# Seven block products in half of the gate/up pieces of a decoder trunk, and low parts made by accumulating transfers

## The chip, the cores and the metric

The kernel runs on one core of one Trainium2 chip. The metric is the device time of one execution in microseconds (us), the median of three runs. Five engines work side by side, each on its own instruction queue: TensorE (matmuls), VectorE, ScalarE, GpSimd (POOL) and SyncE (SP, which here only issues DMAs). Sixteen DMA engines serve the queues of all of them.

## The reference, cut to what matters

Two layers over 256 tokens of width 2048. Layer 0 mixes with a diagonal state-space scan and a gated linear unit, layer 1 with sliding-window attention. Each is followed by a SwiGLU block, which is where the change lies:

```python
def swiglu(x, w_gate, w_up, w_down):
    return (jax.nn.silu(x @ w_gate) * (x @ w_up)) @ w_down
...
        h = h + mix
        hn = rmsnorm(h, norm_ffn[i])
        h = h + swiglu(hn, ffn_w_gate[i], ffn_w_up[i], ffn_w_down[i]).astype(h.dtype)
```

The inner width is 5632. All is float32.

## The kernel before, in words

**Three matmuls for one product.** Every operand is split into a high part, rounded to the matmul's reduced float32 (`F32R`), and a low part, the rest. `products` adds high x high, high x low and low x high into one PSUM bank (L926, L927, L928), 128 x 128 by 128 x 512 each. A *piece* is a block of weights of 512 rows by 512 columns, 1 MB. It takes 4 row blocks x 2 blocks of 128 tokens x 3 = 24 matmuls. The program has 332 pieces: 32 of the gated linear unit, 36 of attention's projections, 88 for gate, 88 for up, 88 for down.

**How a piece gets ready.** The class `Weights` holds the pieces in the order of use. When TensorE's code takes piece i (`next`), the pieces up to i+2 are split and up to i+4 loaded. A load is one DMA issued by SP (L109) into one of two buffers `raw`. `high` (L122) is one ScalarE instruction that writes the rounded copy into a buffer `w`, of which there are three, so a piece's buffer is that of the piece three before it. `low` (L127) is one VectorE subtraction, raw minus high.

**The FFN.** The 5632 inner columns go in 11 chunks of 512. For a chunk, four pieces of gate are multiplied, then four of up (the first chunk alternates between them, so that the last quarter of the normed activations is wanted late). ScalarE applies the gate's function, VectorE multiplies by up, and the result is turned (32 x 32 block transposes on VectorE, `blocks_turned`, L1007) and split into high and low for the down product; each layer's last chunk is turned by TensorE instead. Chunks come in groups of three, and the group's down product (4 blocks of output columns) stands after the first chunk of the next group.

**Order.** Instructions are issued to each engine by a list scheduler which simulates the program and takes what is ready; the code's order is the priority. Work that can be deferred is put into the list `left` and taken out between pieces. PSUM has eight banks, each one accumulator of 128 x 512.

Of the kernel before, what the change touches and what calls it, by code (L numbers as in the profile page):

```python
# [9 lines left out]
F32 = mybir.dt.float32  # L10
# [7 lines left out]
P = 128  # L18
# [4 lines left out]
EPS = 1e-6  # L23
FF = 5632
FFC = FF // 512
FF_GROUPS = ((0, 1, 2), (3, 4, 5), (6, 7, 8), (9, 10))

G = 128
NS = 64
# [27 lines left out]
def kernel(  # L57
# [9 lines left out]
    def nm(s):  # L67
        uid[0] += 1
        return f"{s}_{uid[0]}"
# [10 lines left out]
    def bank(shape, name="ps"):  # L80
        return ps.tile(shape, F32, tag="ps", name=nm(name))
# [5 lines left out]
    def normed_tile(name):  # L87
        return wp.tile([P, 2, 4, T], F32R, tag="xt", name=nm(name), bufs=4)


    class Weights:
        def __init__(self):
            self.src, self.raw, self.hl = [], [], []
            self.early = {}
            self.third = None
            self.used = 0
            self.limit = 0

        def add(self, ap):
            self.src.append(ap)  # L100

        def load(self, upto):
            while len(self.raw) < min(upto, len(self.src)):
                i = len(self.raw)
                if i in self.early:
                    t = self.early[i]()
                else:
                    t = pp.tile([P, 4, 512], F32, tag="raw", name=nm("raw"), bufs=2)
                nc.sync.dma_start(t, self.src[i].rearrange("(a p) n -> p a n", p=P))  # L109
                self.raw.append(t)  # L110

        def place(self, i):
# [12 lines left out]
        def low(self, i, keep=lambda ins: ins, e=V):  # L125
            hi, lo = self.hl[i]
            keep(e.tensor_tensor(lo, self.raw[i], hi.bitcast(F32), op=ALU.subtract))  # L127

        def split(self, upto):
# [17 lines left out]


    TWO_ORDER = [(n, q) for n in (0, 1) for q in range(3)] + [(0, 3), (1, 3)]

    def add_ffn(i):
        def gu(c):
            pairs = [(w, q) for w in (w_gate, w_up) for q in range(4)]
            if c == 0:
                pairs = [((w_gate, w_up)[n], q) for n, q in TWO_ORDER]
            for w, q in pairs:
                W.add(w[i, 512 * q : 512 * (q + 1), 512 * c : 512 * (c + 1)])

        def down(g):
            for n in range(NCH):  # L160
                for c in FF_GROUPS[g]:
                    W.add(w_down[i, 512 * c : 512 * (c + 1), 512 * n : 512 * (n + 1)])

        ffn_order(gu, down)

    def ffn_order(gu, down):
        done = 0
        for g, chunks in enumerate(FF_GROUPS):
            for n, c in enumerate(chunks):
                gu(c)  # L170
                if n == 0 and g > 0:
                    down(g - 1)
        down(len(FF_GROUPS) - 1)
# [815 lines left out]
    def block_tile():  # L989
        return bt_tile().rearrange("p a b -> p (a b)")[:, : 4 * T].rearrange("p (a t) -> p a t", a=4)  # L990
# [3 lines left out]
    def through_dram(o, v):  # L994
# [3 lines left out]
            nc.gpsimd.dma_start(d[t].rearrange("(q k) e -> k q e", q=4), v[32 * t : 32 * t + 32])  # L998
        nc.gpsimd.dma_start(o, d.rearrange("t p e -> p t e"))

    def blocks_turned(o, v, tb):


        src = v[32 * tb : 32 * tb + 32].rearrange("p t (a c) -> p t a c", a=4)
        dst = o.rearrange("p a (t k) -> p t a k", t=2)
        for q in range(4):
            V.transpose(dst[32 * q : 32 * q + 32, :, :, 32 * tb : 32 * tb + 32],  # L1007
                        src[:, :, :, 32 * q : 32 * q + 32])

    class Norm:  # L1010
# [15 lines left out]
        def chunk(self, n, t):  # L1026
            self.square(n, t)
            if t == 1 and n in self.blocks:
                o, v = normed_tile("xT"), block_tile()
                self.xt[n] = o  # L1030
                left.extend(partial(blocks_turned, v, h[:, n], tb) for tb in range(4))

                def split():
                    gc = gcol[:, self.g, 4 * n : 4 * n + 4]
                    for a in range(4):
                        S.activation(o[:, 0, a], v[:, a], AF.Copy, scale=gc[:, a : a + 1])
                        V.scalar_tensor_tensor(o[:, 1, a], v[:, a], gc[:, a : a + 1], o[:, 0, a].bitcast(F32),
                                               ALU.mult, ALU.subtract)

                left.append(split)  # L1040
            elif t == 1 and n in self.through:
                left.extend(self.late)
                v, land = block_tile(), wp.tile([P, 2, 512], F32, tag="act", name=nm("act"), bufs=2)
                o = self.xt[n] = normed_tile("xT")
                V.transpose(v.rearrange("p a t -> p (a t)").rearrange("p (q t a k) -> p t a q k", q=4, t=2, a=4),  # L1045
                            h[:, n].rearrange("p t (a q k) -> p t a q k", a=4, q=4))
                through_dram(land.rearrange("p t c -> p (t c)").rearrange("p (b e) -> p b e", b=4),
                             v.rearrange("p a t -> p (a t)").rearrange("p (q e) -> p q e", q=4))

                lv = land.rearrange("p t c -> p (t c)").rearrange("p (b t a k) -> p b t a k", b=4, t=2, a=4)  # L1050

                def split():
                    gc = gcol[:, self.g, 4 * n : 4 * n + 4]
# [12 lines left out]
            elif t == 1:  # L1066
                left.extend(self.late)
                left.append(lambda: self.xt.__setitem__(n, normed(n, self.g)))

        def scale(self):  # L1070
            s = wp.tile([P, 2], F32, tag="ss", name=nm("ss"), bufs=2)
# [30 lines left out]
    def glu(norm):  # L1102
# [5 lines left out]
        for c in range(NCH):  # L1108
# [11 lines left out]
            for t in range(2):  # L1120
# [4 lines left out]
                V.tensor_tensor(hc, hc, sg, op=ALU.add)  # L1125
                norm.chunk(c, t)

    def swiglu(norm, out_norm):
        ht = {}
        r = [None]  # L1130

        def turned(c, hm):
            o = turned_tile("hT")
            for t in range(2):
                pt = bank([P, 4, P], "tr")
                for a in range(4):
                    PE.transpose(pt[:, a], hm[:, t, a * P : (a + 1) * P], ident)
                ts_ = slice(t * P, (t + 1) * P)
                S.copy(o[:, 0, :, ts_], pt)  # L1139
                V.tensor_tensor(o[:, 1, :, ts_], pt, o[:, 0, :, ts_].bitcast(F32), op=ALU.subtract)  # L1140
            ht[c] = o

        def gu(c):
            last = c == FF_GROUPS[-1][-1]
            if c == 0:
                pg, pu = two_linear(norm.xt)
                r[0] = norm.scale()
            else:
                pg = linear(norm.xt)
            sg = wp.tile([P, 2, 512], F32, tag="act", name=nm("act"), bufs=2)  # L1150
            for t in range(2):
                S.activation(sg[:, t], pg[t], AF.Silu, scale=r[0][:, t : t + 1])
            if c > 0:
                pu = linear(norm.xt)
            for t in range(2):
                V.scalar_tensor_tensor(sg[:, t], pu[t], r[0][:, t : t + 1], sg[:, t], ALU.mult, ALU.mult)
            if last:
                left.append(lambda: turned(c, sg))
                return
            o, v = turned_tile("hT"), block_tile()  # L1160
            ht[c] = o
            left.extend(partial(blocks_turned, v, sg, tb) for tb in range(4))

            def split():
                S.activation(o[:, 0], v, AF.Copy)  # L1165
                V.tensor_tensor(o[:, 1], v, o[:, 0].bitcast(F32), op=ALU.subtract)

            left.append(split)

        def down(g):  # L1170
            xt = Later(ht, FF_GROUPS[g])
            for n in range(NCH):
                last = out_norm.g is None and g == len(FF_GROUPS) - 1 and n == NCH - 1
                acc = linear(xt, len(FF_GROUPS[g]), halves=last)
                for t in range(2):
                    hc = h[:, n, t]
                    V.tensor_tensor(hc, hc, acc[t], op=ALU.add)  # L1177
                    if g == len(FF_GROUPS) - 1:
                        out_norm.chunk(n, t)

        ffn_order(gu, down)

    class Later:
        def __init__(self, d, keys):
# [2 lines left out]
        def __getitem__(self, i):  # L1187
            return self.d[self.keys[i]]

    def attention(norm, out_norm):  # L1190
        with tc.tile_pool(name="at", bufs=1) as ap:

            ji = ap.tile([P, 384], I32, name="ji")
# [153 lines left out]
            for n in range(NCH):  # L1347
                acc = accs[n] if n < 2 else linear(ot, 4)
                for t in range(2):
                    hc = h[:, n, t]  # L1350
                    V.tensor_tensor(hc, hc, acc[t], op=ALU.add)
                    out_norm.chunk(n, t)


    accs = []
# [9 lines left out]

    h = wp.tile([P, NCH, 2, 512], F32, name="h")

    n0 = Norm(0, (0, 1, 2, 3))
    glu(n0)
    n1 = Norm(1, (), (0, 1, 2, 3))  # L1370
    swiglu(n0, n1)
    n2 = Norm(2, (0, 1, 2, 3))
    attention(n1, n2)
    swiglu(n2, Last(None))


_INS = ["x", "norm_mix", "s5_a_re", "s5_a_im", "s5_log_step", "s5_b_re", "s5_b_im", "s5_c_re", "s5_c_im",
# [25 lines left out]
```

## Time and profile before

| | |
|---|---|
| median of 3 runs | 1981.72 us (1980.31 to 1982.71) |
| span of the profiled execution | 1976.9 us |
| median less that span | 4.8 us |
| TensorE busy | 1935.3 us |
| VectorE busy | 1287.2 us |
| ScalarE busy | 859.9 us |
| moved by DMA | 374.23 MB, mean 189 GB/s |
| mean granted TensorE clock | 0.993 |

The span runs from the first to the last instruction of one execution; the run's own time has a few us around it. Busy times are sums of instruction durations on an engine; matmuls overlap in their pipeline, so TensorE's busy time says only when it had work, and the rate is read from how many start in a stretch. Idle time of an engine that is not the bottleneck costs nothing by itself.

### The profile page before, as it was taken

How to read it: one execution, taken by the hardware profiler on the slowest of the kernel's cores; microseconds unless marked ns; L12 is line 12 of the kernel's file. 1: busy time of each engine (PE TensorE's matmuls, PEld its weight loads, DVE VectorE, ACT ScalarE, POOL GpSimd, SP SyncE). 2: the span in 40 equal slices, each digit the busy share in tenths (PEclk: the TensorE clock that was granted, in tenths of full speed). 3: DMA queues.
4: the chain of work that ended last, by engine and by line, in shares of the span. 5: the costliest groups of instructions: out<-in, count | busy, mean ns of one | idle time of the engine just before them, and what ended most of it. 6: DMA issues, size and time to landing. Idle time of an engine off the chain costs nothing.

```text
span 1976.9 us, 24861 instructions
## 1 busy us (share of the span) xinstructions
PE 1935.3 (98%) x10312; PEld 1600.9 (81%) x10312; DVE 1287.2 (65%) x1689; ACT 859.9 (43%) x839; POOL 130.5 (7%) x122
## 2 busy tenths in 40 slices
PE   8699999999999999999999999999999999999998
PEld 6578888888888888888888778888888888888886
DVE  8966667666556656665577888766654665566545
ACT  6554444343334333433455554443333434333333
POOL 6850000000000000000010110000000000000000
PEclk9899999999999999999999999999999999999999
DMA  4037666556666665656585864665566556656664
GB/s 131 24 103 224 209 207 199 182 186 209 192 192 188 195 197 186 201 189 205 176 280 186 261 226 150 195 209 192 191 192 192 191 191 201 195 190 188 205 191 149
DMA packets 188181, 374.23 MB, mean 189 GB/s; under 512 B 11203, under 2 KB 11267, under 8 KB 187941
## 3 DMA queue, kind: packets, MB, share of 16 engines
q1 hardware_dynamic: 183168, 356.87, 56.4%
q0 software_dynamic: 4064, 13.65, 2.1%
q10 hardware_dynamic: 836, 2.14, 0.3%
q8 instruction: 80, 1.31, 0.3%
q14 instruction: 33, 0.26, 0.0%
HBM read 363.72 MB, written 8.91 MB: 188 GB/s over the span
## 4 chain that ended last, share of the span: by engine, by line
PE 91%; DVE 6%; DMA 1%; issue 1%; ACT 1%; POOL 0%; DVEq 0%; POOLq 0%; ACTq 0%
PE acc L926 30%; PE acc L927 29%; PE acc L928 29%; DVE scan L577 1%; DVE V L582 1%; DVE V L580 1%; DVE w L127 1%; PE pv L214 1%; PE py L802 0%; DMA pT<-pd 0%; DMA pd<-bt 0%; PE px L214 0%; DVE bt L1285 0%; DMA raw<-in_attn_w_qkv_dram 0%; ACT w L122 0%
## 5 line engine op out<-in xcount | busy, mean ns | idle before, releaser
L127 DVE TENSOR_TENSOR w<-raw,w 128x2048 fp32r<-128x2048 f32 x330 | 756.9, 2294 | 579.4 <-ACT w L122 577.4
L122 ACT ACTIVATE w<-raw 128x2048 fp32r<-128x2048 f32 x332 | 636.1, 1916 | 840.6 <-PE acc L928 543.1
L926 PE MATMUL acc<-w,xT 128*128 128x512 f32 x1568 | 611.8, 390 | 0.0
L928 PE MATMUL acc<-w,xT 128*128 128x512 f32 x1568 | 611.0, 390 | 0.0
L927 PE MATMUL acc<-w,xT 128*128 128x512 f32 x1568 | 610.9, 390 | 0.0
L926 PEld LDWEIGHTS acc<-w,xT 128*128 128x128 f32 x1568 | 294.5, 188 | 62.4 <-issue 1.8
L928 PEld LDWEIGHTS acc<-w,xT 128*128 128x128 f32 x1568 | 294.5, 188 | 61.4 <-issue 0.3
L927 PEld LDWEIGHTS acc<-w,xT 128*128 128x128 f32 x1568 | 294.5, 188 | 60.7
L926 PE MATMUL acc<-w,hT 128*128 128x512 f32 x704 | 274.6, 390 | 0.0
L927 PE MATMUL acc<-w,hT 128*128 128x512 f32 x704 | 273.9, 390 | 0.0
L928 PE MATMUL acc<-w,hT 128*128 128x512 f32 x704 | 273.6, 390 | 0.0
L926 PEld LDWEIGHTS acc<-w,hT 128*128 128x128 f32 x704 | 132.2, 188 | 28.3 <-ACT hT L1139 1.2
L928 PEld LDWEIGHTS acc<-w,hT 128*128 128x128 f32 x704 | 132.2, 188 | 27.5
L927 PEld LDWEIGHTS acc<-w,hT 128*128 128x128 f32 x704 | 132.2, 188 | 27.2
L1007 DVE STREAM_TRANSPOSE bt<-act 32x256 f32<-32x256 f32 x320 | 139.6, 436 | 5.5
L927 PE MATMUL acc<-w,gt 128*128 128x512 f32 x256 | 99.9, 390 | 0.6 <-DVE w L127 0.6
L926 PE MATMUL acc<-w,gt 128*128 128x512 f32 x256 | 100.0, 391 | 0.0
L928 PE MATMUL acc<-w,gt 128*128 128x512 f32 x256 | 99.8, 390 | 0.0
L998 POOL DMA_DIRECT2D pd<-bt x40 | 21.9, 553 | 932.9 <-DVE bt L1045 842.7
L1165 ACT ACTIVATE hT<-bt 128x1024 fp32r<-128x1024 f32 x20 | 21.2, 1062 | 96.9 <-DVE bt L1007 96.8
L1007 DVE STREAM_TRANSPOSE bt<-h 32x256 f32<-32x256 f32 x128 | 55.8, 436 | 1.9
L1177 DVE TENSOR_TENSOR h<-h,acc 128x512 f32<-128x512 f32 x64 | 43.0, 686 | 21.4 <-PE acc L928 21.4
(249 smaller groups left out, 1283.3 us busy)
## 6 DMA issues: line engine op xcount, KB each, us to landing
raw<-in_ffn_w_gate_dram SPq DMA_DIRECT2D x88, 1024.0 KB, 5.2
raw<-in_ffn_w_up_dram SPq DMA_DIRECT2D x88, 1024.0 KB, 5.2
raw<-in_ffn_w_down_dram SPq DMA_DIRECT2D x88, 1024.0 KB, 5.1
raw<-in_s_w_glu_dram SPq DMA_DIRECT2D x32, 1024.0 KB, 5.4
raw<-in_attn_w_qkv_dram SPq DMA_DIRECT2D x20, 1024.0 KB, 5.2
raw<-in_attn_w_o_dram SPq DMA_DIRECT2D x16, 1024.0 KB, 5.2
pd<-bt POOLq DMA_DIRECT2D x24, 192.0 KB, 4.7
pT<-pd POOLq DMA_DIRECT2D x6, 768.0 KB, 5.8
```

Of the source, the lines that this page charges most:

```text
L122: keep(S.activation(w[:, 0], self.raw[i], AF.Copy))
L127: keep(e.tensor_tensor(lo, self.raw[i], hi.bitcast(F32), op=ALU.subtract))
L214: return (lambda *a, **k: pin(f(*a, **k))) if self.on else f
L577: keep(V.tensor_tensor(t_, ws[..., part], bc(Vt[hf][:, k - 1, :, part], 1, 2), op=ALU.mult))
L580: V.tensor_tensor(v, v, t_[:, 0], op=ALU.add)
L926: keep(PE.matmul(acc, x_[:, 0], w[0][:, a], start=first, stop=False))
L927: PE.matmul(acc, x_[:, 0], w[1][:, a], start=False, stop=False)
L928: PE.matmul(acc, x_[:, 1], w[0][:, a], start=False, stop=last)
L998: nc.gpsimd.dma_start(d[t].rearrange("(q k) e -> k q e", q=4), v[32 * t : 32 * t + 32])
L1007: V.transpose(dst[32 * q : 32 * q + 32, :, :, 32 * tb : 32 * tb + 32], src[:, :, :, 32 * q : 32 * q + 32])
L1165: S.activation(o[:, 0], v, AF.Copy)
L1177: V.tensor_tensor(hc, hc, acc[t], op=ALU.add)
```

## The change

In each chunk the eight pieces are cut differently: piece p holds 256 rows of w_up beside the same 256 rows of w_gate. So a piece is a 2 x 2 arrangement of blocks (two row blocks of 128, two matrices), and the activations are one as well (two blocks of tokens, two row blocks). For p = 0, 2, 4, 6 the eight block products are replaced by seven, by the Strassen-Winograd scheme: sums of weight blocks (t1 to t4) and of activation blocks (s1 to s4) are formed first, and sums of the products afterwards. That takes 21 matmuls instead of 24. VectorE forms the sums of weights in float32 and the low parts; ScalarE the two sets of high parts. The blocks used as they are (b11, b22, b21) go into a buffer `sd` of which there is one.

For p = 1, 3, 5, 7 the piece keeps 24 matmuls, but its low part is made without VectorE: ScalarE writes the high part, then the negated high part into the place of the low part, and two DMAs issued by GpSimd read the raw weights from DRAM a second time and add them to it (`accum_op=add`).

All eight PSUM banks are accumulators of a chunk; four of them (m1, m5, m6, m7) are combined on VectorE during piece 7. The turned result of a chunk now always goes through DRAM: one transpose on VectorE, four DMAs out and one back on GpSimd's queue. Groups of chunks become (0,1), (2,3), (4,5), (6,7), (8,9,10), and half of a group's down product stands after each of the next group's first two chunks. The last group's first two column blocks are accumulated side by side, with the last chunk read last (`LAST_ORDER`). Attention's buffers are given back before its residual additions, and the buffers of the FFN are taken there.

```diff
-FF_GROUPS = ((0, 1, 2), (3, 4, 5), (6, 7, 8), (9, 10))
+FF_GROUPS = ((0, 1), (2, 3), (4, 5), (6, 7), (8, 9, 10))
+SEVEN = (0, 2, 4, 6)
...
+                for s, ap in enumerate(aps):
+                    nc.sync.dma_start(v[:, s], ap.rearrange("(a p) n -> p a n", p=P))
...
+        def sevenths(self, i):
+            self.load(i + 1)
+            r = self.raw[i]
+            w = self.place(i)
+            d = self.pool.tile([P, 2, 3, 512], F32R, tag="sd", name=nm("sd"), bufs=1)
+            f = self.pool.tile([P, 4, 512], F32, tag="sf", name=nm("sf"), bufs=1)
+            V.tensor_tensor(f[:, 0:2], bc(r[:, 0], 1, 2), r[:, 1:3], op=ALU.subtract)
+            V.tensor_tensor(f[:, 2], r[:, 2], f[:, 0], op=ALU.subtract)
+            V.tensor_tensor(f[:, 3], r[:, 3], f[:, 2], op=ALU.subtract)
+            S.activation(w[:, 0], f, AF.Copy)
+            S.activation(d[:, 0], r[:, 1:4], AF.Copy)
+            V.tensor_tensor(w[:, 1], f, w[:, 0].bitcast(F32), op=ALU.subtract)
+            V.tensor_tensor(d[:, 1], r[:, 1:4], d[:, 0].bitcast(F32), op=ALU.subtract)
...
+        def sent(self, i):
+            self.high(i)
+            hi, lo = self.hl[i]
+            S.activation(lo, hi.bitcast(F32), AF.Copy, scale=-1.0)
+            aps = self.src[i][0]
+            v = lo.rearrange("p (k s) n -> p s k n", s=len(aps))
+            for s, ap in enumerate(aps):
+                nc.gpsimd.dma_start(v[:, s], ap.rearrange("(a p) n -> p a n", p=P), accum_op=ALU.add)

         def split(self, upto):
             while len(self.hl) < min(upto, len(self.src)):
-                self.high(len(self.hl))
-                self.low(len(self.hl) - 1)
+                i = len(self.hl)
+                if self.src[i][1]:
+                    self.sevenths(i)
+                elif self.src[i][2]:
+                    self.sent(i)
+                else:
+                    self.high(i)
+                    self.low(i)
...
+            for p in range(8):
+                W.add(*(w[i, 256 * p : 256 * (p + 1), 512 * c : 512 * (c + 1)] for w in (w_up, w_gate)),
+                      seven=p in SEVEN, sent=p not in SEVEN)
...
+        M = {"m1": ("a11", "b11"), "c11": ("a12", "b21"), "c12": ("s4", "b22"), "c21": ("a22", "t4"),
+             "m5": ("s1", "t1"), "m6": ("s2", "t2"), "m7": ("s3", "t3")}
+        FIRST = ("m1", "m6", "m7", "m5", "c11", "c21", "c12")
+        REST = ("m1", "c11", "c12", "m5", "m7", "m6", "c21")
...
+            def sums():
+                S.copy(u[:, 0], acc["m1"])
+                V.tensor_tensor(u[:, 1], u[:, 0], acc["m6"], op=ALU.add)
+                V.tensor_tensor(u[:, 2], u[:, 1], acc["m7"], op=ALU.add)
+                V.tensor_tensor(u[:, 1], u[:, 1], acc["m5"], op=ALU.add)
+                V.tensor_tensor(u[:, 3], u[:, 2], acc["m5"], op=ALU.add)
...
+                if p == SEVEN[-1]:
+                    sums()
...
+            for t, (g, m) in enumerate(((0, "c11"), (2, "c21"))):
+                V.tensor_tensor(u[:, g], u[:, g], acc[m], op=ALU.add)
+                S.activation(sg[:, t], u[:, g], AF.Silu, scale=r[0][:, t : t + 1])
+            for t, (g, m) in enumerate(((1, "c12"), (3, "c22"))):
+                V.tensor_tensor(u[:, g], u[:, g], acc[m], op=ALU.add)
+                V.scalar_tensor_tensor(sg[:, t], u[:, g], r[0][:, t : t + 1], sg[:, t], ALU.mult, ALU.mult)
...
+            def send():
+                lv = moved(sg)
+
+                def split():
+                    for t in range(2):
...
+                        S.activation(hi, v, AF.Copy)
+                        V.tensor_tensor(lo, v, hi.bitcast(F32), op=ALU.subtract)
+
+                left.extend([lambda: None] * 2 + [split])
+
+            left.append(send)
...
+        def last():
+            accs = [[bank([P, 512], "acc") for _ in range(2)] for _ in range(2)]
+            for i, (n, c) in enumerate(LAST_ORDER):
+                piece(accs[n], ht[c], c == FF_GROUPS[-1][0], c == FF_GROUPS[-1][-1])
+                pop_left(3 - i)
```

More of the change, by code (lines that the diff above doesn't have):

```diff
@@ L93, in __init__, with add @@
             self.src, self.raw, self.hl = [], [], []
-            self.early = {}
             self.third = None
+            self.pool = None
             self.used = 0
             self.limit = 0
-        def add(self, ap):
-            self.src.append(ap)
+        def add(self, *aps, seven=False, sent=False):
+            self.src.append((aps, seven, sent))
         def load(self, upto):
@@ L1126, in glu, with pop_left @@
                 norm.chunk(c, t)
+    def pop_left(pieces):
+        for _ in range(-(-len(left) // max(1, pieces))):
+            left.pop(0)()
     def swiglu(norm, out_norm):
@@ L1170, in down, with three @@
-        def down(g):
-            xt = Later(ht, FF_GROUPS[g])
[L1172 to L1181, printed above, removed]
+        def three(acc, x_, w, first, last):
+            PE.matmul(acc, x_[0], w[0], start=first, stop=False)
+            PE.matmul(acc, x_[0], w[1], start=False, stop=False)
+            PE.matmul(acc, x_[1], w[0], start=False, stop=last)
@@ L1183 @@
+        ffn_order(gu, down, last)
     class Later:
@@ L1346, in attention @@
                         f()
[L1347 to L1352, printed above, removed]
+        after()
+        for n in range(NCH):
+            acc = accs[n] if n < 2 else linear(ot, 4)
+            for t in range(2):
+                hc = h[:, n, t]
+                V.tensor_tensor(hc, hc, acc[t], op=ALU.add)
+                out_norm.chunk(n, t)
     accs = []
```

173 lines of the change are left out of this document (104 added, 69 removed).

## The prediction

> **What bounds the kernel now.** I read the page's busy times first, then the chain of work that ended last, then the costliest groups, and after these the stretches of the two FFNs.
>
> ```profile
> span 1976.9 us, 24861 instructions
> PE 1935.3 (98%) x10312; PEld 1600.9 (81%) x10312; DVE 1287.2 (65%) x1689; ACT 859.9 (43%) x839; POOL 130.5 (7%) x122
> ...
> PE 91%; DVE 6%; DMA 1%; issue 1%; ACT 1%; POOL 0%; DVEq 0%; POOLq 0%; ACTq 0%
> ...
> L127 DVE TENSOR_TENSOR w<-raw,w 128x2048 fp32r<-128x2048 f32 x330 | 756.9, 2294 | 579.4 <-ACT w L122 577.4
> L122 ACT ACTIVATE w<-raw 128x2048 fp32r<-128x2048 f32 x332 | 636.1, 1916 | 840.6 <-PE acc L928 543.1
> ```
>
> TensorE carries 91% of the chain. ScalarE's idle time before the high parts (L122) ends mostly with a matmul: ScalarE waits for a weight buffer that TensorE gives back, so the preparation runs ahead. The same in the stretches of the two FFNs (columns: length, busy time and instructions of each engine, granted clock, DMA share, GB/s):
>
> ```profile
> 277.00:960.00 683.00, 683.00 (x3015) 565.87 (x3014) 410.64 (x370) 272.48 (x171) 0.00 (x0) 1.00 0.61 194
> 1232.00:1960.00 728.00, 728.00 (x3216) 602.73 (x3215) 448.78 (x413) 293.92 (x200) 0.00 (x0) 1.00 0.60 193
> ```
>
> TensorE has no gap in either, at granted clock 1.00: 683 / 3015 gives one matmul every 0.2265 us. A piece of 24 takes 5.44 us, two pieces 10.87. The DMA engines are busy 0.61.
>
> **The change part by part.** The sum is made against the profiled span; the median of the runs, 1981.7, lies 4.8 above it, and I add the difference to the median.
>
> *Matmuls removed.* Four of eight gate/up pieces in each of 22 chunks go from 24 to 21 matmuls: 264 x 0.2265 = 59.8 us off TensorE, all on the chain. A pair (one piece of seven products, one "sent" piece) becomes 45 x 0.2265 = 10.19 us; there are 88 pairs. The transposes of each layer's last chunk leave too:
>
> ```profile
> L1137 PE MATMUL tr<-ident,act x16: 270/272/273, 973.8 to 1929.3; 128*128 128x128 f32 x16
> ```
>
> At most 16 x 0.272 = 4.4 us, at least 0; I take 2, since they are pipelined.
>
> *VectorE and ScalarE.* Prices by size (128 partitions):
>
> ```profile
> L1165 ACT ACTIVATE hT<-bt 128x1024 fp32r<-128x1024 f32 x20 | 21.2, 1062 | 96.9 <-DVE bt L1007 96.8
> L1166 DVE TENSOR_TENSOR hT<-bt,hT 128x1024 fp32r<-128x1024 f32 x20 | 24.5, 1225 | 20.3 <-ACT hT L1165 20.3
> L1177 DVE TENSOR_TENSOR h<-h,acc 128x512 f32<-128x512 f32 x64 | 43.0, 686 | 21.4 <-PE acc L928 21.4
> L1156 DVE SCALAR_TENSOR_TENSOR act<-acc,ry,act 128x512 f32<-128x512 f32 x44 | 31.5, 750 | 10.9 <-PE acc L928 10.9
> L1152 ACT ACTIVATE act<-acc,ry 128x512 f32<-128x512 f32 x44 | 30.1, 688 | 53.8 <-PE acc L928 53.8
> L1007 DVE STREAM_TRANSPOSE bt<-act 32x256 f32<-32x256 f32 x320 | 139.6, 436 | 5.5
> L1285 DVE STREAM_TRANSPOSE bt<-sc 128x1536 f32<-128x1536 f32 x6 | 10.6, 1773 | 0.0
> ```
>
> A seven-product piece costs VectorE 1.23 + 2 x 0.69 for the sums of blocks, 2.29 for low parts of four sums and about 1.76 (between the 1024 and 2048 rows) for three blocks: 6.66 us; ScalarE 1.92 + 1.49. A sent piece costs VectorE nothing and ScalarE 2 x 1.92. Turning a chunk loses 16 x 0.436 of VectorE and gains one transpose of about 1.2 and two splits of 0.69; eight additions of 0.69 join them. Per chunk VectorE goes from 8 x 2.29 + 16 x 0.436 + 1.23 + 2 x 0.75 = 28.0 of 43.5 us to 4 x 6.66 + 8 x 0.69 + 2 x 0.75 + 1.2 + 2 x 0.69 = 36.2 of 40.8; ScalarE from 8 x 1.92 + 2 x 0.69 + 1.06 = 17.8 to 4 x 3.41 + 8 x 1.92 + 5 x 0.69 = 32.5. Neither sum passes TensorE's, so I book 0; but VectorE at 89% can't absorb much lateness. Bounds at a chunk's end: the four "m" banks are emptied under piece 7 and cost 0; an evacuation queued behind one 2.29 us operation costs TensorE up to 2.3, 50 us over 22 chunks. I take 0, since 12 matmuls (2.7 us) on emptied banks stand first in the next chunk.
>
> *The wait that the change adds.* A sent piece D needs the weight buffer that the piece three before it, a seven-product piece A, gives back. When A ends, ScalarE has in its queue: high parts of three blocks of piece C between them (one buffer, also held by A; 1.49), high part of D (1.92), its negation (1.92). Only then does POOL issue the accumulating transfer: 5.4 us after A. Behind these on ScalarE stand the next chunk's copies and gates. TensorE meanwhile has sent piece B (5.44) and seven-product piece C (4.76), 10.19 us. So the transfer has 4.8 us to land. If it takes X, each sent piece starts S late; over two of them 2S = 5.4 + X - 10.2, hence S = (X - 4.8) / 2 and a pair takes 10.19 + S. It equals the 10.87 of before at S = 0.68, X = 6.2.
>
> No transfer of this kind is in the trace. Nearest rows:
>
> ```profile
> q1 hardware_dynamic: 183168, 356.87, 56.4%
> ...
> raw<-in_ffn_w_gate_dram SPq DMA_DIRECT2D x88, 1024.0 KB, 5.2
> ...
> pT<-pd POOLq DMA_DIRECT2D x6, 768.0 KB, 5.8
> ...
> pd<-bt POOLq DMA_DIRECT2D x16, 128.0 KB, 4.6
> act<-pd POOLq DMA_DIRECT2D x4, 512.0 KB, 4.7
> ```
> ```profile
> L998 POOL DMA_DIRECT2D pd<-bt x40: 551/551/566, 986.1 to 1159.4; - x40
> L999 POOL DMA_DIRECT2D pT<-pd x6: 757/757/760, 1089.0 to 1163.9; - x6
> ```
>
> Queue q1 used 0.564 x 1976.9 = 1115 us of all engines for 356.87 MB: 3.28 us for a piece of 1.05 MB, so 1.9 of the 5.2 are fixed. Low end: a transfer like a raw load with nothing beside it, and the second half issued some 0.65 later: X = 5.85, S = 0.53, 88 x (10.19 + 0.53 - 10.87) = -13 us. But it isn't alone. The two raw buffers come free 3.4 us after A (C's last low part, D's high part), so two raw loads, 6.55 us of engine time, start 2 us before it. At half the rate one pass lasts 6.55: X = 1.9 + 0.65 + 6.55 = 9.1, S = 2.15, a pair 12.34, +1.47 x 88 = +129 us. The same X = 9.1 follows if the addition needs two passes and nothing runs beside it. High end: two passes and the raw loads, under the rivals. I take 9.1, as the loads beside it are certain, by the raw row.
>
> In the Trainium skill, "DMA: Bandwidth & Descriptors", the table of measured loads under Bandwidth gives 6.15 us for a plain 1 MB load issued from GpSimd; by that figure as X, S would be 0.68 and the change worth nothing. No run here shows it.
>
> *Other queues and edits.* SP issues a gate/up piece as two DMAs instead of one, off the chain:
>
> ```profile
> L109 SPq DMA_DIRECT2D raw<-in_ffn_w_gate_dram x88: 367/368/378, 277.0 to 1878.6; - x88
> ```
>
> 0.37 us more of SP per piece, for 5.1 us of TensorE: 0. A chunk's way through DRAM: transpose 1.2, four issues 2.2, landing 4.6, issue 0.76, landing 4.7, in all 13.5 us, on POOL behind up to one accumulating transfer (9.1). Its first reader, in the last group, comes four pieces (21.8 us) later: 0; if that cover goes, a few us twice. Five groups instead of four add 16 additions of 0.69 on VectorE, beside TensorE: 0. The forms of the normed activations are wanted in the order of quarters, the last after six pieces as now: 0. Attention's moved pool: 0.
>
> Sum: 1981.7 + 129 - 2 = 2109 us.
>
> **The rivals.**
>
> *The other side: the transfers land in time.* The raw loads give way or finish early and X stays under 6.2; at X = 4.8 all of 59.8 + 2 is gained: 1920, at X = 5.85 some 1967. For it: 5.2 us in the raw row, and DMA engines idle 0.39 of the FFN now. Also, if ScalarE takes D's high part ahead of C's blocks, the transfer has 6.3 us. Against it: engine time per pair rises from 6.55 to at least 9.8 + 0.8 (a chunk's way through DRAM moves 1 MB, a quarter per pair) of 10.2.
>
> *The addition is two passes, and DMA the bound.* The destination must be read as well as the source. A pair then holds 6.55 + 6.55 + 0.8 = 13.9 us of engine time: +3.0 x 88 = +266, 2248 us; with S from X = 13.5, +3.67 x 88 = +323. What speaks for a better price is the best short window (last columns: DMA share and GB/s):
>
> ```profile
> 634.00:636.00 2.00, 2.00 (x10) 1.69 (x9) 1.26 (x2) 1.93 (x2) 0.00 (x0) 1.00 1.01 393
> ```
>
> At 393 GB/s the 4.46 MB (2.1 of raw loads, 2 x 1.05, 0.26 through DRAM) would take 11.4, only +43. The rule is in the Trainium skill too: "Collectives: The Full Stack", Part 3, says that an adding transfer issues two source reads on one ring and so runs at half the rate of a copy. No run here shows it.
>
> *The raw loads become late instead.* With one buffer of blocks, the chain from A's end to the next seven-product piece but one is 1.49 + 1.76 + raw load + 2.6 + 1.92 + 2.29; TensorE reaches that piece after three others.
>
> ```profile
> DMA to landing us min/median/max: 4.9/5.2/9.1
> ```
>
> With 5.2 the chain is 15.6 with handovers; a pair takes (15.6 + 4.76) / 2 = 10.2, no loss. It costs from a landing of 6.8 on; at 9.1 a pair takes 12.1: 2088 us. That can be so with the accumulating transfers hidden.
>
> *Far worse:* an addition of more than two passes, or a granted clock that falls in the gaps: over 2310.
>
> **How the numbers follow.** Forecast (sent pieces late by some 2 us) 0.30, own range 2000 to 2200; two passes and DMA-bound 0.25; raw loads late 0.10; over 2310 0.07; hidden, faster 0.24; within 0.2% 0.04 (runs spread 1980.3 to 1982.7, so 0.2%, 4 us, is about what can be told from no change). Slower adds to 0.72. The range 1930 to 2310 leaves out the far-worse case and the part of the faster case with nearly all of the saving.
>
> **What would show it.** Right: 3960 gate/up matmuls over both layers instead of 4224; TensorE idle before matmuls that read sent pieces, ended by the accumulating transfer, near 2 us each; its landing near 9 us; ScalarE's high parts waiting for TensorE less. Wrong: landings under 6 us, with TensorE still without gaps and pairs of 10.2 us; or gaps ended by VectorE's low parts or at chunk starts; or DMA share at 1.0 through the gate/up pieces, which is the two-pass case.

## The result and the profile after

The changed kernel takes 2136.9 us (median, 2126.3 to 2141.0) against 1981.4 us (1980.3 to 1982.7) for the kernel before, measured beside it: a ratio of 1.0781 [1.0753, 1.0809], 155.5 us slower. The profiled execution has a span of 2132.8 us, 155.9 more than the 1976.9 of before. The page of the changed kernel, in the order in which the page of before was read:

```profile
span 2132.8 us, 25785 instructions
PE 1948.2 (91%) x10032; PEld 1573.6 (74%) x10032; DVE 1465.1 (69%) x1891; ACT 1159.1 (54%) x1065; POOL 411.3 (19%) x408
...
q1 hardware_dynamic: 185984, 356.88, 49.0%
q0 software_dynamic: 59328, 129.01, 30.3%
...
PE 43%; DMA 31%; DVE 12%; ACT 7%; issue 5%; POOL 1%; SPq 0%; DVEq 0%; ACTq 0%; POOLq 0%
...
L1232 PE MATMUL acc<-w,xT 128*128 128x512 f32 x2112 | 544.5, 409 | 125.9 <-DMA w<-in_ffn_w_gate_dram 121.3
...
L155 POOL DMA_DIRECT2D w<-in_ffn_w_up_dram x88 | 105.8, 1202 | 1016.1 <-ACT w L151 799.7
...
L155 POOL DMA_DIRECT2D w<-in_ffn_w_gate_dram x88 | 149.8, 1702 | 0.0
...
raw<-in_ffn_w_up_dram SPq DMA_DIRECT2D x176, 512.0 KB, 4.8
raw<-in_ffn_w_gate_dram SPq DMA_DIRECT2D x176, 512.0 KB, 6.1
...
w<-in_ffn_w_up_dram POOLq DMA_DIRECT2D x88, 512.0 KB, 7.0
w<-in_ffn_w_gate_dram POOLq DMA_DIRECT2D x88, 512.0 KB, 9.3
```

There are 280 matmuls fewer (264 and the 16 transposes). TensorE's share of the chain falls from 91% to 43% and DMA's rises from 1% to 31%. The group L1232 is the matmuls of the sent pieces; the last two fields are TensorE's idle time before them and what ended it: 121.3 of 125.9 us ended with the second half of an adding transfer (its up half is issued first, its gate half second). That half lands 9.3 us after its issue.

One sent piece in the timeline (columns: start and length in us, engine, line; in brackets the idle time before and what ended it), first ScalarE and POOL, then TensorE:

```profile
637.75 1.49 ACT L141 ACTIVATE sd<-raw 128x1536 fp32r<-128x1536 f32 x1 [3.32 <-PE acc L1197]
...
640.52 1.92 ACT L123 ACTIVATE w<-raw 128x2048 fp32r<-128x2048 f32 x1 [1.29 <-PE acc L1197]
642.35 1.90 ACT L140 ACTIVATE w<-sf 128x2048 fp32r<-128x2048 f32 x1
644.15 1.90 ACT L151 ACTIVATE w<-w 128x2048 fp32r<-128x2048 f32 x1
...
646.77 1.20 POOL L155 DMA_DIRECT2D w<-in_ffn_w_up_dram  x1 [9.62 <-PE acc L1197]
```
```profile
650.67 3.79 PE L1232 MATMUL acc<-w,xT 128*128 128x512 f32 x16
656.13 2.06 PE L1232 MATMUL acc<-w,xT 128*128 128x512 f32 x8 [1.67 <-DMA w<-in_ffn_w_gate_dram]
```

The high part (L123) is ready at 642.4, its negation (L151) at 646.05, because the next piece's high parts of sums (L140) stand between them. The second half lands some 10 us after the negation. TensorE does not stop at the start of the piece: it multiplies 16 times with the high part and stops before the 17th matmul, the first that reads the low part.

The stretches of the changed kernel (columns as before: length, busy time of each engine, granted clock, DMA share, GB/s): seven chunks with their down products, the down pieces behind one chunk, eight chunks of the other layer; then one chunk's gate/up pieces, twice.

```profile
539.00:1030.00 491.00, 455.46 (x1919) 366.04 (x1918) 320.73 (x282) 267.18 (x174) 94.39 (x98) 0.98 0.90 252
588.00:610.00 22.00, 22.00 (x99) 18.22 (x98) 16.52 (x17) 12.82 (x10) 3.34 (x6) 1.00 0.75 247
1503.00:2056.00 553.00, 503.79 (x2111) 404.44 (x2110) 353.28 (x313) 296.36 (x192) 98.34 (x99) 0.97 0.90 250
```
```profile
539.00:588.00 49.00, 43.78 (x182) 34.63 (x181) 31.17 (x27) 27.34 (x18) 9.75 (x8) 0.97 0.98 254
680.00:729.00 49.00, 43.37 (x180) 34.63 (x179) 28.59 (x25) 26.61 (x16) 9.79 (x8) 0.97 0.98 256
```

The 180 matmuls of a chunk's gate/up pieces would take 40.8 us at 0.2265; they take 49. There the DMA engines are busy 0.98; in the down pieces behind them TensorE has no gap and the DMA engines fall to 0.75.

Summed from the trace's matmul starts, less 0.2265 us each: the sent pieces lose 174 us (133 of them before the 17th matmul), the seven-product pieces 34. With the 59.8 saved, -60 + 174 + 34 = +148 of the 155.9. Not all of these 208 us are waits: some 39 us are 189 matmuls that follow each other without a gap, but slower, in short stretches at half the granted clock, such as this one (8 matmuls started in 3.4 us; at 0.2265 it would be 15):

```profile
562.30:565.70 3.40, 3.26 (x8) 2.62 (x9) 1.55 (x2) 0.47 (x1) 2.43 (x2) 0.50 1.05 404
```

The mean granted clock is 0.970 in this execution and 0.993 before. From a chunk's first gate/up matmul to its last it is 50.2 us in the mean over the 22 chunks, against 43.5 before.

### The profile page after: what moved, and what is told of

Its sections match the earlier page's. It is cut to its first block, busy times and chain, and to the rows that moved or that the text cites. A ratio compares the mean times of both kernels' runs of the same rounds, so it can differ in the third digit from the quotient of the medians.

```text
span 2132.8 us, 25785 instructions
## 1 busy us (share of the span) xinstructions
PE 1948.2 (91%) x10032; PEld 1573.6 (74%) x10032; DVE 1465.1 (69%) x1891; ACT 1159.1 (54%) x1065; POOL 411.3 (19%) x408
## 3 DMA queue, kind: packets, MB, share of 16 engines
q1 hardware_dynamic: 185984, 356.88, 49.0%
q0 software_dynamic: 59328, 129.01, 30.3%
## 4 chain that ended last, share of the span: by engine, by line
PE 43%; DMA 31%; DVE 12%; ACT 7%; issue 5%; POOL 1%; SPq 0%; DVEq 0%; ACTq 0%; POOLq 0%
DMA w<-in_ffn_w_gate_dram 21%; PE acc L1232 8%; PE acc L966 8%; PE acc L967 8%; PE acc L968 8%; DMA raw<-in_ffn_w_gate_dram 3%; DVE w L128 3%; PE acc L1195 3%; PE acc L1196 3%; PE acc L1197 3%; ACT w L123 3%; DMA raw<-in_ffn_w_down_dram 3%; ACT w L140 2%; ACT w L151 1%; DVE scan L617 1%
## 5 line engine op out<-in xcount | busy, mean ns | idle before, releaser
L123 ACT ACTIVATE w<-raw 128x2048 fp32r<-128x2048 f32 x244 | 467.1, 1914 | 423.0 <-DMA raw<-in_ffn_w_down_dram 122.9
L1232 PE MATMUL acc<-w,xT 128*128 128x512 f32 x2112 | 544.5, 409 | 125.9 <-DMA w<-in_ffn_w_gate_dram 121.3
L1232 PEld LDWEIGHTS acc<-w,xT 128*128 128x128 f32 x2112 | 408.9, 197 | 242.2 <-issue 73.3
L128 DVE TENSOR_TENSOR w<-raw,w 128x2048 fp32r<-128x2048 f32 x154 | 352.6, 2290 | 158.7 <-ACT w L123 157.2
L142 DVE TENSOR_TENSOR w<-sf,w 128x2048 fp32r<-128x2048 f32 x88 | 201.7, 2292 | 182.7 <-ACT w L140 182.6
L140 ACT ACTIVATE w<-sf 128x2048 fp32r<-128x2048 f32 x88 | 167.8, 1906 | 117.9 <-DVE sf L139 105.3
L143 DVE TENSOR_TENSOR sd<-raw,sd 128x1536 fp32r<-128x1536 f32 x88 | 154.5, 1756 | 50.0 <-ACT sd L141 49.8
L151 ACT ACTIVATE w<-w 128x2048 fp32r<-128x2048 f32 x88 | 167.6, 1904 | 1.0
L155 POOL DMA_DIRECT2D w<-in_ffn_w_gate_dram x88 | 149.8, 1702 | 0.0
L1196 PE MATMUL acc<-w,xT 128*128 128x512 f32 x352 | 140.8, 400 | 4.4 <-DVE w L142 4.4
L1197 PE MATMUL acc<-w,xs 128*128 128x512 f32 x352 | 140.5, 399 | 0.0
L1195 PE MATMUL acc<-w,xT 128*128 128x512 f32 x352 | 133.9, 396 | 2.7 <-ACT w L140 2.7
```

The costliest lines, as they stand in the source:

```text
L123: keep(S.activation(w[:, 0], self.raw[i], AF.Copy))
L140: S.activation(w[:, 0], f, AF.Copy)
L142: V.tensor_tensor(w[:, 1], f, w[:, 0].bitcast(F32), op=ALU.subtract)
L155: nc.gpsimd.dma_start(v[:, s], ap.rearrange("(a p) n -> p a n", p=P), accum_op=ALU.add)
L1195: PE.matmul(acc, x_[0], w[0], start=first, stop=False)
L1196: PE.matmul(acc, x_[0], w[1], start=False, stop=False)
```

## The experiments

Theories to be told apart after the result. *Lateness*: the transfers start too late. *Rate*: the transfers and the raw loads beside them take more DMA time than there is. *Raw loads*: the seven-product pieces' own way (raw load, sums, high and low parts) is too long. Times are medians; every ratio is to the kernel before, run beside it.

**1. Earlier start.** A sent piece's high part no longer waits for a seven-product piece's buffer; the seven-product pieces share the third one.

```diff
-            pool, n = (wp, 1) if i % 3 == 1 else (wq, 2)
+            pool, n = (wp, 1) if seven or (not sent and i % 3 == 1) else (wq, 2)
```


> Same work and same transfers; only which weight buffer a gate/up piece takes: seven-product pieces always the one of `wp`, sent pieces the two of `wq` in turn. So a sent piece's high part waits for the sent piece two before it, a whole piece (4.8 us) earlier than now. Theory 'lateness' (the accumulating transfer starts too late, and lands 10.3 us after the negation where 8.4 would do): the budget grows to 13.2, the gaps inside sent pieces mostly go, 1930 to 1990 us. Theory 'rate' (the DMA engines are full: 0.96 busy in a gate/up stretch, because the addition takes two passes): a stretch of 50 us can fall to 48 at most, 2090 to 2140 us, DMA share 0.97 or more.

2147.6 us, 1.0854 [1.0818, 1.0890]. The negation now ends 11.0 us ahead of the 17th matmul instead of 10.5, and the second half lands 10.8 us after it instead of 10.3 (medians over the 88 pieces): what was gained ahead was lost in the transfer. The gain is small in any case: counted to the time at which the 17th matmul would follow the 16th without a wait, it is 1.0 us (9.8 instead of 8.8). Summed from the matmul starts as above, the waits before the 17th matmul fall from 133 to 112 us, and the seven-product pieces, which now share one buffer, lose 54 instead of 34 (its profiled execution has a span of 2157.6 us). So the run gives to one side and takes from the other, and does not rule lateness out.

**2. The same transfers without the addition.** They overwrite instead of adding.

```diff
-    nc.gpsimd.dma_start(v[:, s], ..., accum_op=ALU.add)
+    nc.gpsimd.dma_start(v[:, s], ...)
```


> The same transfers without the addition: they overwrite the negated high part with the raw weights, so the low parts of sent pieces are left out. If the addition reads twice, GpSimd's queue falls from 30% of the engines' span to 17 to 19%, a pair asks for 10.0 us of engine time instead of 12.9, and the time comes to 1930 to 1980 us (both 'rate' and 'lateness' with two passes). If an adding transfer costs no more than a plain one and it is only its start that is late: queue share as before, 2110 to 2140 us.

2012.8 us, 1.0164 [1.0142, 1.0185]: 124 us come back, fewer than either theory's 1930 to 1980 us asked for. The queue of GpSimd's transfers and the matmuls of the sent pieces, and the stretch of one chunk:

```profile
q0 software_dynamic: 59328, 129.01, 21.1%
...
L1232 PE MATMUL acc<-w,xT 128*128 128x512 f32 x2112 | 510.5, 394 | 36.9 <-DMA w<-in_ffn_w_gate_dram 34.3
```
```profile
583.00:626.00 43.00, 41.63 (x180) 33.43 (x179) 27.59 (x23) 26.15 (x17) 5.54 (x8) 1.00 0.88 286
```

Same packets, same bytes counted, but 21.1% of 2015.5 = 425 us of all engines instead of 30.3% of 2132.8 = 646. Idle time ended by the transfer falls from 121 to 34 us.

**3. No transfers.**

```diff
-    for s, ap in enumerate(aps):
-        nc.gpsimd.dma_start(v[:, s], ..., accum_op=ALU.add)
```


> The accumulating transfers are left out; the low part of a sent piece stays the negated high part. Both theories: the seven-product pieces and all the rest run without gaps, 1915 to 1940 us, DMA share 0.65 to 0.7. The rival 'raw loads and VectorE' (gaps that remain when the transfers are gone, since VectorE has 36 of 40.8 us in a chunk and one block buffer): over 1960 us.

1998.0 us, 1.0083 [1.0066, 1.0101]. Missed: with no transfer at all the kernel is still slower than before, 81 us above the 1977 - 60 = 1917 that 264 fewer matmuls would give. Where the idle time is now (groups by form, then waits):

```profile
L1228 PE MATMUL acc<-w,xT 128*128 128x512 f32 x2112 | 496.2, 390 | 1.2 <-ACT w L123 1.2
L1192 PE MATMUL acc<-w,xT 128*128 128x512 f32 x352 | 143.6, 408 | 16.2 <-DVE w L142 16.0
L1192 PE MATMUL acc<-sd,xT 128*128 128x512 f32 x264 | 106.6, 404 | 18.1 <-DVE sd L143 18.1
```
```profile
ACT sd L141 <- DMA raw<-in_ffn_w_gate_dram: 155.8, 51, 7.0
DVE sf L137 <- DMA raw<-in_ffn_w_gate_dram: 120.4, 58, 5.9
```
```profile
q0 software_dynamic: 11456, 36.73, 5.7%
...
raw<-in_ffn_w_up_dram SPq DMA_DIRECT2D x176, 512.0 KB, 4.0
raw<-in_ffn_w_gate_dram SPq DMA_DIRECT2D x176, 512.0 KB, 5.5
```

The sent pieces (L1228) have no gaps. The seven-product pieces do: TensorE waits for VectorE's low parts, but ScalarE and VectorE had themselves waited for the raw load, 156 and 120 us in all. So the releaser that the group names (VectorE) need not be the cause; the wait ahead of it can be. Run 7 tests that.

**4. Low parts of the sent pieces on GpSimd** instead of transfers: the negation and the transfers go, `self.low(i, e=PL)` comes.

> The low part of a sent piece by a subtraction on GpSimd (4.6 us for this shape in the trace of before) instead of negation and transfers; all is computed. Both theories: DMA back to 0.65 to 0.7, GpSimd 4.6 of 10.2 us per pair, ScalarE 1.9 us per pair less: 1920 to 1945 us, faster than the kernel before. The rival 'shared port' (VectorE slowed while GpSimd subtracts; one subtraction took 2.89 instead of 2.29 us before): VectorE up to 42 us in a chunk of 40.8, 1960 to 2010 us.

2217.8 us, 1.1201 [1.1181, 1.1221], the slowest of all and far above both forecasts. Groups of this kernel, and below them VectorE's 128x512 subtraction in the changed kernel:

```profile
L128 POOL TENSOR_TENSOR w<-raw,w 128x2048 fp32r<-128x2048 f32 x89 | 426.7, 4795 | 906.6 <-ACT w L123 880.2 <-DVE xT L1120 11.2 <-DVE hT L1254 8.3
L142 DVE TENSOR_TENSOR w<-sf,w 128x2048 fp32r<-128x2048 f32 x88 | 304.6, 3461 | 214.2 <-ACT w L140 214.1
L1191 PE MATMUL acc<-w,xT 128*128 128x512 f32 x352 | 167.8, 477 | 107.8 <-DVE w L142 107.8
L1254 DVE TENSOR_TENSOR hT<-act,hT 128x512 fp32r<-128x512 f32 x44 | 88.3, 2043 | 15.0 <-ACT hT L1253 14.7
```
```profile
L1259 DVE TENSOR_TENSOR hT<-act,hT 128x512 fp32r<-128x512 f32 x44 | 28.8, 688 | 13.3 <-ACT hT L1258 13.1
```

While GpSimd subtracts, VectorE's subtractions take longer: 3.46 instead of 2.29 us (L142) and 2.04 instead of 0.69. TensorE then waits 108 us for the seven-product pieces' low parts. So this does not measure the seven products alone; run 5 does.

**5. Seven-product pieces alone:** the four others get their low part from VectorE, as in the kernel before (`self.high(i)`, `self.low(i)`).

> One part of the change alone: the seven block products stay, and the low parts of the four other pieces are again one VectorE subtraction (2.29 us); no negation, no accumulating transfer. Theory 'rate' (the transfers fill the DMA engines and cost 139 us; the other 77 us that the seven products fail to bring come from the way raw weights take to a seven-product piece): near the kernel with its transfers left out, 1990 to 2030 us, DMA share 0.6, gaps at low parts of seven-product pieces. Rival 'VectorE is the bound': 36 us and 9.2 more per chunk against 40.8 of TensorE, 45.4 x 22 = 1000 us of chunks at least, 2030 to 2080 us, with VectorE 0.9 or more busy in a chunk's stretch.

2005.6 us, 1.0134 [1.0118, 1.0151]: 26 us slower than before instead of 60 faster, with no transfer in it.

**6. Transfers alone:** no piece has seven products. This and runs 8, 11 and 12 share an edit that lets a piece be ordinary (24 matmuls, VectorE's low part):

```diff
-SEVEN = (0, 2, 4, 6)
+SEVEN = ()
+SENT = (1, 3, 5, 7)
...
-                      seven=p in SEVEN, sent=p not in SEVEN)
+                      seven=p in SEVEN, sent=p in SENT)
...
+            if 2 * n in SEVEN:
+                first, e0 = self.seven_forms(gc, o, v), None
+            else:
+                first, e0 = None, plain(blocks[1], 0)
```


> The other part alone: pieces 0, 2, 4, 6 of a chunk keep all eight block products (24 matmuls, low part by VectorE), pieces 1, 3, 5, 7 get their low parts by the accumulating transfers. TensorE needs 10.87 us per pair. Theory 'rate': the DMA engines set the pace as in the changed kernel, 48 to 50 us a chunk against 43.5, DMA share 0.95 or more, 2090 to 2140 us, although TensorE has 60 us more work than there. Rival 'the seven products make it late': VectorE is far lighter here (2.29 instead of 6.66 us per pair), so 1980 to 2030 us.

2007.3 us, 1.0140 [1.0111, 1.0169]. The rate theory had said 2090 to 2140 and missed. Seven chunks with their down products, and the page:

```profile
510.00:960.00 450.00, 449.51 (x1978) 370.46 (x1977) 183.88 (x141) 226.74 (x138) 86.39 (x86) 1.00 0.97 273
```
```profile
q0 software_dynamic: 59328, 129.01, 32.5%
...
L1244 PE MATMUL acc<-w,xT 128*128 128x512 f32 x4224 | 968.3, 390 | 14.7 <-DMA w<-in_ffn_w_gate_dram 14.0
```

TensorE has next to no gap in those chunks, while the DMA engines are busy 0.97. (The loss lies mostly in the first four chunks of one layer and the first three of the other, whose gate/up pieces take 44.7 to 47.6 us instead of 43.5.) A chunk with its down product is 192 + 96 matmuls, 65.2 us; so its transfers and loads need 0.97 x 65.2 = 63.2 us of all engines. In the changed kernel a chunk comes every 70.7 us (from the 539 to 963 of its starts, six chunks) at a share of 0.90: 63.6 us, the same work. With 180 + 96 matmuls TensorE needs 62.5. So the two are nearly equal: spread evenly, the DMA work would by this estimate cost about 1 us a chunk, and here it is not spread evenly (0.98 in gate/up, 0.75 behind).

**7. No raw loads for the sent pieces,** and no transfers: they read the raw weights of the piece before them.

```diff
+                if sent:
+                    self.raw.append(self.raw[-1])
+                    continue
```


> The accumulating transfers are left out as in the third run, and also the raw loads of sent pieces, which take their high part from the seven-product piece's raw weights before them. So both raw buffers serve seven-product pieces and a load can start a pair earlier. Theory 'raw loads late': the 77 us that the third run still lost go, 1920 to 1945 us. Rival 'VectorE and ScalarE': their work is that of the third run, and so is the time, 1985 to 2000 us.

1935.9 us, 0.9777 [0.9761, 0.9793].

```profile
640.00:681.00 41.00, 41.00 (x182) 33.79 (x181) 28.39 (x24) 25.19 (x16) 2.18 (x4) 1.00 0.49 166
```

A chunk's gate/up pieces take 41 us without a gap, though VectorE, ScalarE and TensorE do the same as in run 3. So 62 of run 3's 81 us were the raw loads of the sent pieces, by their DMA time or by the buffers that they hold (the run takes away both); the engines' own work was not in the way of these. The exception is the first chunk of the second layer's FFN, 49.0 us here:

```profile
1224.00:1273.00 49.00, 44.84 (x182) 35.32 (x181) 45.38 (x64) 40.02 (x32) 0.00 (x0) 0.93 0.27 88
```

VectorE, which also makes the seven forms of the activations there, is busy 45.4 of the 49 us. Run 8 has 49.8 us for this chunk against 42.4 for the others.

**8. Two seven-product pieces of eight,** six ordinary, no transfers: `SEVEN = (0, 4)`, `SENT = ()`.

> Seven products in pieces 0 and 4 of a chunk alone; the six others keep 24 matmuls and a low part by one VectorE subtraction; no accumulating transfer. TensorE loses 132 matmuls, 29.9 us. VectorE 2 x 6.66 + 6 x 2.29 + 9.6 = 36.7 of 42.1 us per chunk. If raw loads are what holds seven-product pieces back, three ordinary pieces between them give the time back: 1950 to 1970 us, faster than the kernel before. If VectorE's load does: 1980 to 2010 us.

1959.4 us, 0.9895 [0.9880, 0.9910]: faster than both kernels, by 20 of the 29.9 us that 132 fewer matmuls can give. Nothing of the computation is left out in it.

**9. The changed kernel with a third raw buffer,** for every third piece; small scratch tiles share places to make room.

```diff
+                own = i % 3 == 1 and (32 <= i < 164 or i >= 200)
+                pool, tag, n = (self.pool, "raw3", 1) if own else (pp, "raw", 2)
```


> The changed kernel with a third buffer for raw weights (room for it from scratch tiles that now share one place; the work and the bytes are the same). Transfers alone needed 44.5 us a chunk with the same bytes, so the DMA engines' own floor is at most that. Theory 'the two parts meet in the raw loads' (the transfers make raw loads late, and with two raw buffers a late load holds the next seven-product piece and the next load): chunks of 50.2 us fall to 44.5 to 46, 2010 to 2050 us. Rival 'the engines are simply full' (0.986 busy in a chunk's stretch): 2110 to 2145 us.

2099.2 us, 1.0606 [1.0545, 1.0667]: 38 us better than the changed kernel, between both forecasts (2010 to 2050 and 2110 to 2145). Inconclusive by itself. A window over seven chunks:

```profile
535.00:1000.00 465.00, 436.98 (x1882) 352.71 (x1881) 313.57 (x277) 266.43 (x171) 87.19 (x90) 1.00 0.94 262
```

The DMA share rises from 0.90 to 0.94 and a chunk comes every 68.3 us (535 to 945, six chunks): 64.2 us of engine time, again the same work, spread a little more evenly.

**10. Run 5 with the third raw buffer.**

> Seven products in four pieces, no transfers (low parts by VectorE), and the third raw buffer. Theory 'raw loads late' (as the run with shared raw weights showed with its transfers left out): the 4 us a chunk go, 1925 to 1960 us. Rival 'VectorE': 45.4 us of work for 40.8 of TensorE in a chunk, which the lighter down pieces can take only in part: 1980 to 2010 us.

1987.9 us, 1.0038 [1.0024, 1.0051], 18 us better than run 5. This lies in the range of the rival that VectorE holds it (1980 to 2010), not in that of the raw loads (1925 to 1960). Seventeen of the 22 chunks take 41.3 to 42.4 us where 180 matmuls are 40.8, although VectorE makes the low parts of all eight pieces. But the first and third of each layer take 51 to 62, and one later chunk 45. The first three chunks of layer 0, and seven later ones with their down products:

```profile
294.00:438.00 144.00, 133.39 (x541) 104.69 (x540) 129.29 (x132) 74.78 (x60) 6.08 (x10) 0.94 0.54 186
523.00:966.00 443.00, 442.29 (x1936) 362.96 (x1935) 378.34 (x309) 216.79 (x146) 20.58 (x35) 1.00 0.65 216
```

No down product stands between the first three chunks, and VectorE is busy 0.90 of the time; later, with down products between, 0.85, and TensorE has next to no gap. That points at VectorE in the early chunks, which no run here tests; the granted clock is lower there too. The scratch tiles that now share places can't be all of it: run 5 doesn't share them and has 51 us in each layer's third chunk and 57 in the second layer's first.

**11. Three seven-product pieces and the third raw buffer:** `SEVEN = (0, 2, 4)`, `SENT = ()`.

> Seven products in pieces 0, 2 and 4, the other five ordinary, no transfers, third raw buffer. 198 matmuls fewer, 44.9 us. VectorE 3 x 6.66 + 5 x 2.29 + 9.6 = 41.0 of 41.4 us in a chunk, with slack in the down pieces. If raw loads were the only hold: 1935 to 1948 us, the fastest yet; if VectorE's load holds it: 1955 to 1980 us.

1964.0 us, 0.9922 [0.9906, 0.9937]: no better than two pieces with two buffers, and again in the range of the rival that VectorE holds it. Most chunks take 41.8 to 41.9 us where 183 matmuls are 41.4; the second layer's first takes 51.5.

**12. Neither part:** `SEVEN = ()`, `SENT = ()`; the new order of pieces, groups, turning and attention stays.

> Neither part: all eight pieces of a chunk keep 24 matmuls and a low part by VectorE; what is left of the change is the rest (pieces of up and gate side by side, results turned through DRAM, new groups, all eight banks as accumulators). It says what the two parts are to be measured against. By the prediction the rest costs nothing: 1976 to 1984 us. If the first chunk of the second layer waits in it as it does in every run so far (48 to 65 us instead of 43.5): 1984 to 1995 us.

1976.9 us, 0.9987 [0.9977, 0.9997]; every chunk's gate/up pieces take 43.5 us, the second layer's first too. The rest of the change costs nothing, and the wait in that chunk, which every run with seven products has, belongs to these.

**The account.** From run 12's 1977, 264 matmuls less give 1917. Seven-product pieces that get ready late add 81 (run 3): 62 go without the sent pieces' raw loads (run 7), and about 8 of the other 19 lie in the first chunk of the second layer. The adding transfers add 139 more (run 3 to the changed kernel), of which 124 go when nothing is added (run 2). The two parts meet: alone, against run 12, the seven-product pieces cost 29 (run 5) and the transfers 30 (run 6), together 160. Both want the DMA engines and the raw buffers in the same 41 us; that this is why they cost more together is argued, as no run separates the two.

## Why the prediction was right, and where its steps were not

Direction, size (2109 forecast, 2136.9 measured) and place were right: gaps stand before the matmuls of sent pieces, ended by the adding transfer. But the wait itself is smaller than forecast: 133 / 88 = 1.51 us a piece stand before the 17th matmul, against S = 2.15. Less the 59.8 saved, that is +73 us, not +129. Another 74 are in terms that the sum had at 0: 34 in the seven-product pieces and 40 in the rest of the sent ones (27 of these are matmuls at half the clock). So the closeness of the size is partly luck; the direction and the wait are not.

**The budget.** The prediction counted the time until TensorE *starts* the sent piece: 4.8 us. TensorE stops before the 17th matmul, so 16 x 0.2265 = 3.6 us more are covered, 8.4 in all. With the forecast's X = 9.1 the formula would then have given S = 0.35 and a gain of some 30 us. The right size came from errors the other way in the next points.

**The transfer's length.** X was 9.1 as one pass at half rate beside raw loads; measured from the negation's end, the second half lands after 10.3 us (median; 8.7 to 13.5). The work is more than one pass. Over the 88 pieces: (646 - 114) / 88 = 6.05 us of all engines for one adding 1 MB transfer, where 114 = 5.7% of run 3's 2000 us is the queue's other traffic; run 2's plain one is (425 - 114) / 88 = 3.5, and a raw load of SyncE's queue takes 0.49 x 2132.8 / 356.88 x 1.05 = 3.07. So an addition costs 1.7 to 2 times a copy. That is the price of the rival "two passes" (6.55). In the Trainium skill, "Collectives: The Full Stack", Part 3, the half rate by two source reads, stated there for the additions of a reduce-scatter, agrees with it: 6.05 against 3.07 to 3.5 here.

**Is it the two-pass rival, then?** By its own sign, a DMA share of 1.0 in the gate/up pieces, in large part yes: 0.98. Its time, 2248, was too high because it set 13.9 us of engine time against one pair. A chunk's down product has its TensorE time too, into which part of the loading can move: run 6 carries the same bytes at 10.87 us a pair. Taken over chunk and down product, the floor is 63 to 64 us against TensorE's 62.5. The forecast's case (sent pieces late by about 2 us) and this rival were not exclusive; I had priced them as if they were.

**Raw loads late**, given 0.10 and said to cost "from a landing of 6.8 on". Runs 3 and 7 show them costing 62 us at a median landing of 5.5. Two things were missing from that chain: the raw buffer isn't free when the load is wanted, since a seven-product piece holds it through sums and low parts (in run 3 the load queue waits 338 us, 58 times, for the last sum of weights), and a median is not what TensorE waits for: the longest single wait for a raw load is 7.0 us. In the changed kernel this is hidden in part, since TensorE is already late by the transfers: the seven-product pieces lose 34 us there, 70 in run 3.

**The order on ScalarE.** I had blocks' high part, D's high part, negation in a row, 5.4 us from A's end. In the timeline the blocks' high part is written before A ends (its buffer is read early in A), but the next sums' high part (1.90) stands between high part and negation: 5.7 us from A's end, by other steps; the median over 66 pieces (those whose A is in the same chunk) is 6.5. With 6.5, 10.3 and the 3.6 us more of cover, the prediction's formula gives S = (6.5 + 10.3 - 13.8) / 2 = 1.5, the 1.51 measured. So the form of the wait was right and its sizes were off. And POOL needs 1.20 and 1.70 us for the two issues, where I took 0.65 from rows of smaller transfers.

**VectorE, and the forms of the activations,** both at 0. In most chunks VectorE is no bound: in run 10's chunks of 41.3 us it does even more than here. But runs 10 and 11 came out where VectorE's load was forecast to put them, their early chunks are slow with VectorE busy 0.90, and the forms that were to cost 0 come with about 8 us in the second layer's first chunk (49.0 and 49.8 us in runs 7 and 8, against 41.2 and 42.4 for the others).

**What held.** The reorganization costs nothing (run 12). 3960 gate/up matmuls are there (2112 + 1848).

**What stays open.** How the 139 us of the transfers split between low parts that land late and raw loads that they delay: an earlier start gave nothing in all (run 1, which made the seven-product pieces later), a third raw buffer 38 us (run 9), dropping the addition 124 (run 2), and these are not independent. Why single chunks early in a layer are slow in runs 5 and 9 to 11, where VectorE's load is the likeliest cause. And what brings on the stretches at half the clock.

## What to carry to other kernels

Work taken off a busy engine by a DMA has to be paid in DMA engine time over the whole period, with the loads beside it, and an adding transfer counts 1.7 to 2 times here. Before fewer matmuls are bought with more preparation, follow the feed back to the buffer of the raw operand: two seven-product pieces of eight gained 1%, four with the same two buffers lost 1.3%. And count a wait from the first instruction that reads the operand, not from the start of the piece.

## What the runs showed of the hardware

An adding transfer of 512 KB occupies GpSimd for 1.20 to 1.70 us at its issue, a copying one of the same shape for 0.71 (run 2, both halves). While GpSimd subtracts with both inputs in SBUF, VectorE's subtractions of that kind take 1.5 to 3 times as long (2.29 to 3.46 us, 0.69 to 2.04 us). The Trainium skill, "SBUF — State Buffer", "Who interferes with whom", says that a VectorE instruction with two SBUF inputs contends with a GpSimd instruction that reads SBUF; run 4 agrees, with these numbers. The granted clock of the changed kernel is 0.97 in the gate/up pieces with their gaps and 1.00 in the down pieces; the 0.97 is a mean of 1.00 and of short stretches at 0.50. But seven chunks of run 9, with 28 us of gaps in 465, have 1.00, so gaps alone don't explain these stretches.
